# Three 256-column products in place of a 512 and a 256, and a sum taken out by ScalarE alone

## The chip, the cores and the metric

The kernel runs on one core of a Trainium2 chip. The metric is the device time of one execution in microseconds; lower is better. The kernel before takes 1694.68 us in the median of three runs (1694.48 to 1695.0). Numbers of the trace come from one profiled execution of it.

## The reference

One layer of a hybrid decoder trunk on x of 256 positions and 2048 features, all in float32:

```
h = x @ w_in                      # 2048 x 14352, columns for three branches and three gates
y_a = s5_branch(...)              # diagonal complex state space model, then z * sigmoid(z @ w_glu + b_glu)
y_b = gla_branch(...)             # gated linear attention, 4 heads
y_c = hgrn2_branch(...)           # f = lb + (1 - lb) * sigmoid(f_logit), q = silu(q), 8 heads
merged = sum_b sigmoid(gate_b) * (y_b @ w_up_b)
x = layer_norm(alpha * x + merged @ w_out)
x = layer_norm(alpha * x + square(relu(x @ w_mlp_in)) @ w_mlp_out)
```

The hidden width of the MLP is 8192. A layer is done once. Nearly all of the arithmetic lies in the products with the weight matrices.

## The kernel before

**Products in two parts.** Every float32 operand of a large product is split into a coarse part (hi, rounded to the type fp32r) and the rest (lo). A product is the sum of three: hi·hi, hi·lo and lo·hi. ScalarE makes hi by a copy, VectorE makes lo by a subtraction (both 128x1024 elements for one weight tile, L129 and L107 in the profile, since one helper records all activations and one all additions of two tensors).

**Chunks.** The program is a list of chunks, each 512 columns ("rows") or 256 columns ("cols") of one weight matrix. A chunk of kind "rows" keeps positions on the partitions: the activations are the stationary operand and the weights move, 512 columns at a time, in three matmuls (L1327, L1328, L1329). A chunk of kind "cols" gives its result transposed, output columns on partitions and the 256 positions along the bank: the weights are stationary and the activations move. A tile of activations holds hi and lo side by side, 256 columns each, so `a[2]` is both (512 columns), `a[0]` is hi and `a[1]` is lo. One step on 128 rows of the contraction was two matmuls, L1332 and L1333:

```
T.matmul(ps, lhsT=wh[:, i, n], rhs=a[2], start=f, stop=False)
T.matmul(ps[:, 0:256], lhsT=wl[:, i, n], rhs=a[0], start=False, stop=l)
```

The first puts hi·hi into columns 0 to 255 of a PSUM bank and hi·lo into columns 256 to 511; the second adds lo·hi to columns 0 to 255. The two halves still had to be added when the bank was taken out: that is `joined`, a copy of the right half by ScalarE and an addition of the left half by VectorE. A function (Silu, Sigmoid, Relu) followed half a step later on ScalarE, over the tile in SBUF.

**Which chunks are transposed.** The inputs of S5 (four chunks), keys and queries of the GLA branch (two and two), forget gates and queries of the HGRN branch (four and four), all with a contraction of 2048; the four chunks of the S5 gate `w_glu` (contraction 1024); and all of the MLP's first product but its first 512 columns (30 chunks, contraction 2048). A chunk has two result tiles (t = 0 and 1). That makes 100 tiles. One more chunk of kind "low" uses L1332 and L1333 too and is not changed.

**Order.** One loop goes over all steps (a quarter of a chunk's contraction or an eighth, for one t). In each step it first issues splits some steps ahead, takes out finished banks (`evacuate`), issues weight loads, runs side tasks, and then issues the step's matmuls. Side tasks (the S5 scan, the attention of the other branches, what follows a bank taken out) are generators; those of lower priority run only while two running sums, estimated VectorE and ScalarE time (`used["v"]`, `used["s"]`, filled by the helpers `tt`, `stt`, `act` and lowered by 1240 a step), are below zero. So an operation that is no longer issued lets tasks run earlier. Each engine then works off its instructions in the order of issue. Three banks serve as accumulators, five after the S5 scan is done. `joined` took a buffer of the pool of 18 half pages, which the S5 tasks use as well.

Of the kernel before, what the change touches and what calls it, by code (L numbers as in the profile page):

```python
# [55 lines left out]
def trunk_kernel(ctx: ExitStack, tc, io, out):  # L56
# [27 lines left out]
    def half(shape=(128, 2, 256), dt=F32):  # L84
        return take("hf", shape, dt)
# [34 lines left out]
    def act(o, a, f, bias=None, scale=None, accum=None):  # L120
        used["s"] += size(a) / 1.3 + 180
        kw = {}
        if bias is not None:
            kw["bias"] = bias
        if scale is not None:
            kw["scale"] = scale
        if accum is not None:
            kw["accum_out"] = accum
        S.activation(o, a, f, **kw)  # L129
# [590 lines left out]
            act(R[key, c][:, t, :], ps, func, scale=scale)  # L720
        return f

    def joined(ps, o, scale=None):

        b = half((128, 2, 256))
        act(b[:, 0, :], ps[:, 256:512], AF.Copy, scale=scale)
        if scale is None:
            tt(o, ps[:, 0:256], b[:, 0, :], ALU.add)
        else:
            stt(o, ps[:, 0:256], scale, b[:, 0, :], ALU.mult, ALU.add)  # L730
        free(b)

    def ev_page(key, i, func=None, scale=None):

        def f(t, ps):
            n = 2 * i + t
            if n == 0:
                R[key] = page()
            o = R[key][:, n, :]
            joined(ps, o, scale)  # L740

            def later():
                yield 0.5
                if func is not None:
                    act(o, o, func)
                if n == 3:
                    yield 0.5
                    R[key, "ok"] = True
            spawn(later(), -1)
        return f  # L750

    def room(tag, n, reserve=4):
# [69 lines left out]
    def ev_f(g, i):  # L822

        def f(t, ps):
            n = 2 * i + t
            if n == 0:
                R["fA", g], R["fK", g] = page(), page()
            hd = 4 * g + n
            A, K = R["fA", g][:, n, :], R["fK", g][:, n, :]
            joined(ps, K)  # L830

            def later():
                yield 0.5
                act(K, K, AF.Sigmoid)
                yield 0.5
                ts(A, K, S5["oml"][:, hd:hd + 1], S5["lb"][:, hd:hd + 1], ALU.mult, ALU.add)
                ts(K, A, -1.0, 1.0, ALU.mult, ALU.add)
                if n == 3:
                    R["f", g] = True
            spawn(later(), -1)  # L840
        return f
# [176 lines left out]
    def ev_mlp1(hc, i):  # L1018

        def f(t, ps):  # L1020
            n = 2 * i + t
            if n == 0:
                hid[hc] = page(dt=F32R), page(dt=F32R)
            hi, lo = (p[:, n, :] for p in hid[hc])
            a = half()
            h = a[:, 0, :]
            joined(ps, h)

            def later():
                yield 0.5  # L1030
                act(h, h, AF.Relu)
                act(h, h, AF.Square)
                act(hi, h, AF.Copy)
                yield 0.5
                tt(lo, h, hi.bitcast(F32), ALU.subtract)
                free(a)
            spawn(later(), -1)
        return f
# [102 lines left out]
    def ev_glu(c, i):  # L1141
        def f(t, ps):
            n = 2 * i + t
            if n == 0:
                yT.setdefault("A", {})[c] = (page(dt=F32R), page(dt=F32R))
            hi, lo = (p[:, n, :] for p in yT["A"][c])
            sg = half()
            g = sg[:, 0, :]
            joined(ps, g)
            b = 4 * c + n  # L1150

            def later():
                yield 0.5
                act(g, g, AF.Sigmoid, bias=S5["bglu"][:, b:b + 1])
                yield 0.5
                tt(g, g, zT[c][:, n, :], ALU.mult)
                yield 0.5
                act(hi, g, AF.Copy)
                yield 0.5
                tt(lo, g, hi.bitcast(F32), ALU.subtract)  # L1160
                free(sg)
                if c == 1 and n == 3:
                    free(*zT.values())
            spawn(later(), -1)
        return f
# [122 lines left out]
    for s, (c, ku, j, t) in enumerate(steps):  # L1288
        now[0] = s
        if id(c) not in started:  # L1290
            started.add(id(c))
            for f in hooks.get(id(c), []):
                f()
        old = split_n[0]
        early = ln_from - 8 <= s < ln_from + 12
        kept = max(0, 8 - len(x1q)) if early and s >= ln_from else 0
        while (split_n[0] < len(order) and first_use[split_n[0]] <= s + (14 if early else 2 if s < 14 else LA + 4 * (s > 660))
               and len(live["pg"]) + 2 + kept <= limit["pg"]):
            emit_split()
        if early:  # L1300
            emit_lower(split_n[0])
        evacuate()
        fetch()
        run_tasks(1240, 1240)
        emit_lower(old if s >= 10 else split_n[0])
        if s < 14 and t == 1:
            x_piece(s // 2 + 1)
        k = c.index[ku, j]
        if k not in sps:
            emit_split()  # L1310
        emit_lower(k + 1)
        hi, lo = sps[k]
        kpu = c.kpu
        nk = len(c.units) * kpu
        if t not in c.ps:
            c.ps[t] = c.ps[0] if c.kind == "low" and t else accumulator()
        ps = c.ps[t]
        nj = kpu // 2
        wn = c.units[0].shape[2]
        wh, wl = (a.rearrange("p a b -> p (a b)").rearrange("p (k n) -> p k n", n=wn) for a in (hi, lo))  # L1320
        for i in range(nj):
            kt = ku * kpu + j * nj + i
            f, l = kt == 0, kt == nk - 1
            a = c.act(kt)
            if c.kind == "rows":
                sl = slice(t * 128, (t + 1) * 128)
                T.matmul(ps, lhsT=a[0][:, sl], rhs=wh[:, i, :], start=f, stop=False)  # L1327
                T.matmul(ps, lhsT=a[0][:, sl], rhs=wl[:, i, :], start=False, stop=False)  # L1328
                T.matmul(ps, lhsT=a[1][:, sl], rhs=wh[:, i, :], start=False, stop=l)  # L1329
            elif c.kind == "cols" or i // (nj // 2) == t:  # L1330
                n = slice(t * 128, (t + 1) * 128) if c.kind == "cols" else slice(0, 128)
                T.matmul(ps, lhsT=wh[:, i, n], rhs=a[2], start=f, stop=False)  # L1332
                T.matmul(ps[:, 0:256], lhsT=wl[:, i, n], rhs=a[0], start=False, stop=l)  # L1333
        uses_left[k] -= 1
        if uses_left[k] == 0:
            free(*sps.pop(k))
        if ku == len(c.units) - 1 and j == 1 and (c.kind != "low" or t == 1):
            done.append((c, t, ps))
# [55 lines left out]
```

## Time and profile before

| what | value |
|---|---|
| median of three runs | 1694.68 us |
| the profiled execution's own time | 1694.67 us |
| its span, first to last instruction | 1692.9 us |
| granted TensorE clock, mean | 0.996 |
| HBM read | 308.71 MB |
| weight tiles of 512 KB fetched by SyncE from w_in, w_mlp_in, w_mlp_out, w_up, w_out, w_glu | 224, 128, 128, 48, 32, 8 |

The time of the profiled execution is 1.8 us more than its span and 0.01 us under the median. A row of a group of instructions gives: line, engine, operation, output<-input tiles, shapes, count, then busy time in us and mean ns of one, then the idle time of the engine just before them with what ended it. A row of the timeline gives start and length in us. PE is TensorE's matmuls, PEld its weight loads, DVE VectorE, ACT ScalarE. The ends of matmuls are modelled; their starts are what can be compared. `acc` is an accumulator bank, `pg` a page of SBUF, `hf` a half page, `m` and `pb` banks of side tasks.

### The profile page before, as it was taken

Reading aid. Unit: us, or ns where it says so; the run is one execution under the profiler, and the core shown is the slowest. Engines: PE = TensorE matmul, PEld = TensorE weight load, DVE = VectorE, ACT = ScalarE, POOL = GpSimd, SP = SyncE. Lnnn points to the kernel's source line nnn. Section 1 sums busy time; section 2 is a strip of 40 time slices with the busy share of each in tenths; the row PEclk is TensorE's granted clock in tenths of the full one; section 3 lists DMA queues with packets and bytes.
Section 4 is the critical chain, followed back from the end, with each engine's and each line's share of the span. In section 5 each row is a group of like instructions: output and inputs, shape, how many; then the busy total and the mean of one; then the engine's idle time right before and its main releaser. Section 6 shows DMA issues by size and latency. Waiting matters only on the chain.

```text
span 1692.9 us, 24205 instructions
## 1 busy us (share of the span) xinstructions
PE 1669.5 (99%) x9390; PEld 1385.6 (82%) x9390; DVE 1196.9 (71%) x1586; ACT 826.0 (49%) x1166; POOL 166.3 (10%) x121
## 2 busy tenths in 40 slices
PE   8999999999999999999999999999999999999996
PEld 6888888887877877878888888888888888888885
DVE  5978889698999999985675667555455555555556
ACT  4463554464545444435554466454454545454540
POOL 3132211021322322100000000000000000000000
PEclk9999999999999999999999999999999999999998
DMA  9855565555555665766686555656656565656661
GB/s 289 255 160 170 166 178 173 159 166 163 173 179 150 222 188 165 244 199 196 189 278 210 171 162 157 196 178 191 199 187 210 168 207 166 219 173 203 205 216 50
DMA packets 222899, 318.70 MB, mean 188 GB/s; under 512 B 13204, under 2 KB 122128, under 8 KB 222784
## 3 DMA queue, kind: packets, MB, share of 16 engines
q1 hardware_dynamic: 218448, 309.45, 58.6%
q10 hardware_dynamic: 3568, 6.46, 1.3%
q0 software_dynamic: 768, 1.25, 0.5%
q8 instruction: 74, 1.21, 0.3%
q14 instruction: 41, 0.34, 0.1%
HBM read 308.71 MB, written 2.10 MB: 184 GB/s over the span
## 4 chain that ended last, share of the span: by engine, by line
PE 91%; DVE 5%; ACT 1%; DMA 1%; issue 1%; SPq 0%; DVEq 0%; ACTq 0%
PE acc L1332 21%; PE acc L1327 19%; PE acc L1328 19%; PE acc L1329 19%; PE acc L1333 10%; DVE pg L107 2%; DMA pg<-in_w_in_dram 1%; DVE hf L107 1%; PE m L554 1%; ACT pg L129 1%; PE m L134 1%; DVE pg L118 1%; ACT hf L129 1%; PE m L625 1%; PE pb L510 0%
## 5 line engine op out<-in xcount | busy, mean ns | idle before, releaser
L129 ACT ACTIVATE pg<-pg 128x1024 fp32r<-128x1024 f32 (+2 forms) x604 | 603.4, 1028 | 416.5 <-DVE pg L107 131.9
L107 DVE TENSOR_TENSOR pg<-pg,pg 128x1024 fp32r<-128x1024 f32 (+3 forms) x646 | 752.5, 1192 | 65.4 <-ACT pg L129 39.5
L1327 PE MATMUL acc<-pg,pg 128*128 128x512 f32 x1504 | 595.4, 396 | 4.2 <-ACT pg L129 3.6
L1328 PE MATMUL acc<-pg,pg 128*128 128x512 f32 x1504 | 587.7, 391 | 1.1 <-DVE pg L107 1.1
L1329 PE MATMUL acc<-pg,pg 128*128 128x512 f32 x1504 | 587.2, 390 | 0.3 <-DVE pg L107 0.2
L1332 PE MATMUL acc<-pg,pg 128*128 128x512 f32 x1552 | 551.2, 400 | 0.0
L1333 PE MATMUL acc<-pg,pg 128*128 128x256 f32 x1552 | 436.2, 281 | 0.0
L1332 PEld LDWEIGHTS acc<-pg,pg 128*128 128x128 f32 x1552 | 292.2, 188 | 72.4 <-issue 0.7
L1327 PEld LDWEIGHTS acc<-pg,pg 128*128 128x128 f32 x1504 | 282.9, 188 | 68.2 <-issue 5.4
L1329 PEld LDWEIGHTS acc<-pg,pg 128*128 128x128 f32 x1504 | 282.7, 188 | 61.1 <-DVE pg L107 1.1
L1328 PEld LDWEIGHTS acc<-pg,pg 128*128 128x128 f32 x1504 | 283.1, 188 | 59.5 <-DVE pg L107 4.0
L1333 PEld LDWEIGHTS acc<-pg,pg 128*128 128x128 f32 x1552 | 293.9, 189 | 0.7 <-DVE pg L107 0.2
L129 ACT ACTIVATE hf<-acc 128x256 f32<-128x256 f32 (+2 forms) x103 | 39.9, 387 | 186.1 <-PE acc L1333 177.7
L107 DVE TENSOR_TENSOR pg<-pg,acc 128x512 f32<-128x512 f32 x56 | 38.3, 684 | 123.0 <-PE acc L1329 123.0
L107 DVE TENSOR_TENSOR hf<-acc,hf 128x256 f32<-128x256 f32 (+1 forms) x69 | 29.1, 421 | 134.6 <-ACT hf L129 134.6
L107 DVE TENSOR_TENSOR hf<-hf,hf 128x512 f32<-128x512 f32 (+1 forms) x144 | 117.3, 833 | 3.5 <-ACT hf L129 1.4
L129 ACT ACTIVATE hf<-hf 128x256 f32<-128x256 f32 (+1 forms) x152 | 67.7, 455 | 2.1 <-DMA hf<-pg 0.2
L129 ACT ACTIVATE pg<-acc 128x512 f32<-128x512 f32 x40 | 23.8, 594 | 77.9 <-PE acc L1329 77.8
L107 DVE TENSOR_TENSOR hf<-pb,hf 128x256 f32<-128x256 f32 x128 | 46.4, 414 | 19.1 <-PE pb L510 13.3
L107 DVE TENSOR_TENSOR pg<-hf,pg 128x256 fp32r<-128x256 f32 x84 | 34.7, 422 | 27.7 <-ACT pg L129 27.6
L129 ACT ACTIVATE pg<-m 128x512 fp32r<-128x512 f32 (+2 forms) x35 | 19.7, 562 | 66.2 <-PE m L134 47.1
L484 POOL TENSOR_TENSOR hf<-pg 128x512 f32<-128x512 f32 x16 | 19.8, 1238 | 303.4 <-PE pb L510 85.9
(127 smaller groups left out, 665.9 us busy)
## 6 DMA issues: line engine op xcount, KB each, us to landing
pg<-in_w_in_dram SPq DMA_DIRECT2D x224, 512.0 KB, 4.2
pg<-in_w_mlp_in_dram SPq DMA_DIRECT2D x128, 512.0 KB, 4.6
pg<-in_w_mlp_out_dram SPq DMA_DIRECT2D x128, 512.0 KB, 4.1
pg<-in_w_up_dram SPq DMA_DIRECT2D x48, 512.0 KB, 4.7
pg<-in_w_out_dram SPq DMA_DIRECT2D x32, 512.0 KB, 5.1
pg<-in_s_w_glu_dram SPq DMA_DIRECT2D x8, 512.0 KB, 4.8
hf<-pg SPq DMA_DIRECT2D x96, 32.0 KB, 2.1
hf<-hf SPq DMA_DIRECT2D x96, 32.0 KB, 1.9
```

Of the source, the lines that this page charges most:

```text
L107: V.tensor_tensor(o, a, b, op=op)
L118: V.scalar_tensor_tensor(o, a, s, b, op0=op0, op1=op1)
L129: S.activation(o, a, f, **kw)
L134: T.transpose(ps[:, i * 128:(i + 1) * 128], s, ident)
L484: G.tensor_tensor(co, coarse(cs), fine(cs), op=ALU.mult)
L554: T.matmul(yps[r, 0:256], lhsT=W[:, 2 + ri, r], rhs=m[:, i, :], start=ri == 0, stop=ri == 1)
L625: T.matmul(ps[32 * c:32 * c + 32, i * 16:(i + 1) * 16], lhsT=Kf[:, r], rhs=q4[:, :, 1, :], start=True, stop=True)
L1327: T.matmul(ps, lhsT=a[0][:, sl], rhs=wh[:, i, :], start=f, stop=False)
L1328: T.matmul(ps, lhsT=a[0][:, sl], rhs=wl[:, i, :], start=False, stop=False)
L1329: T.matmul(ps, lhsT=a[1][:, sl], rhs=wh[:, i, :], start=False, stop=l)
L1332: T.matmul(ps, lhsT=wh[:, i, n], rhs=a[2], start=f, stop=False)
L1333: T.matmul(ps[:, 0:256], lhsT=wl[:, i, n], rhs=a[0], start=False, stop=l)
```

## The change

In "cols" chunks the step's two matmuls become three of 256 columns, all into columns 0 to 255 of the bank: hi·hi, hi·lo (the same stationary weights `wh` again) and lo·hi. The bank then holds the finished sum in 256 columns, and `joined` is gone: ScalarE takes the tile out of PSUM in one activation with the function it needs, straight to its place. The part of each `later` task that applied the function, and the half step before it, are gone too.

```diff
-    def joined(ps, o, scale=None):
-
-        b = half((128, 2, 256))
-        act(b[:, 0, :], ps[:, 256:512], AF.Copy, scale=scale)
-        if scale is None:
-            tt(o, ps[:, 0:256], b[:, 0, :], ALU.add)
-        else:
-            stt(o, ps[:, 0:256], scale, b[:, 0, :], ALU.mult, ALU.add)
-        free(b)
-
-    def ev_page(key, i, func=None, scale=None):
+    def ev_page(key, i, func=AF.Copy, scale=None):
...
-            o = R[key][:, n, :]
-            joined(ps, o, scale)
...
+            act(R[key][:, n, :], ps[:, 0:256], func, scale=scale)
+            if n == 3:
+                R[key, "ok"] = True
...
-            joined(ps, K)
+            act(K, ps[:, 0:256], AF.Sigmoid)
...
-            joined(ps, h)
+            act(h, ps[:, 0:256], AF.Relu)
 
             def later():
-                yield 0.5
-                act(h, h, AF.Relu)
                 act(h, h, AF.Square)
                 act(hi, h, AF.Copy)
...
-            joined(ps, g)
             b = 4 * c + n
+            act(g, ps[:, 0:256], AF.Sigmoid, bias=S5["bglu"][:, b:b + 1])
...
-                T.matmul(ps, lhsT=wh[:, i, n], rhs=a[2], start=f, stop=False)
-                T.matmul(ps[:, 0:256], lhsT=wl[:, i, n], rhs=a[0], start=False, stop=l)
+                o = ps[:, 0:256]
+                if c.kind == "cols":
+                    T.matmul(o, lhsT=wh[:, i, n], rhs=a[0], start=f, stop=False)
+                    T.matmul(o, lhsT=wh[:, i, n], rhs=a[1], start=False, stop=False)
+                else:
+                    T.matmul(ps, lhsT=wh[:, i, n], rhs=a[2], start=f, stop=False)
+                T.matmul(o, lhsT=wl[:, i, n], rhs=a[0], start=False, stop=l)
```

TensorE at the end of one transposed chunk and the start of the next, with the first matmul group of the S5 scan (L510, into the banks `pb`) between them. In the other rows the first tile after the arrow is a page of activations, the second a page of weights (1053 and 1081 hold hi before, 1195 and 1229 now; the others lo). Before:

```order
L1332 MATMUL acc_1072<-pg_349,pg_1053 128x512
L1333 MATMUL acc_1072<-pg_349,pg_1054 128x256
L510 MATMUL pb_0_1178<-hf_1094,hf_1095 128x256 x2
L510 MATMUL pb_1_1179<-hf_1094,hf_1095 128x256 x2
L1332 MATMUL acc_1200<-pg_111,pg_1081 128x512
L1333 MATMUL acc_1200<-pg_111,pg_1082 128x256
```

And now:

```order
L1310 MATMUL acc_1216<-pg_349,pg_1195 128x256
L1311 MATMUL acc_1216<-pg_349,pg_1195 128x256
L1314 MATMUL acc_1216<-pg_349,pg_1196 128x256
L510 MATMUL pb_0_1346<-hf_1246,hf_1247 128x256 x2
L510 MATMUL pb_1_1347<-hf_1246,hf_1247 128x256 x2
L1310 MATMUL acc_1371<-pg_111,pg_1229 128x256
L1311 MATMUL acc_1371<-pg_111,pg_1229 128x256
L1314 MATMUL acc_1371<-pg_111,pg_1230 128x256
```

Each pair of 512 and 256 columns is a triple of 256; the columns streamed stay 768, the instructions go from two to three, each with its own load of weights. This first group of the scan stands where it stood.

ScalarE, where the two tiles of a chunk of the MLP's first product are taken out. Rows of `pg` from `pg` with 128x1024 are splits of weights, rows from `hf` work on the hidden tile. Before:

```order
L129 ACTIVATE hf_10320<-acc_10241 128x256
L129 ACTIVATE pg_10332<-pg_10231 128x1024
L129 ACTIVATE hf_10336<-acc_10251 128x256
L129 ACTIVATE hf_10319<-hf_10319 128x256 x2
L129 ACTIVATE pg_10317<-hf_10319 128x256
L129 ACTIVATE hf_10335<-hf_10335 128x256 x2
L129 ACTIVATE pg_10317<-hf_10335 128x256
```

And now:

```order
L129 ACTIVATE hf_10975<-acc_10869 128x256
L129 ACTIVATE hf_10975<-hf_10975 128x256
L129 ACTIVATE pg_10973<-hf_10975 128x256
L129 ACTIVATE pg_10992<-pg_10859 128x1024
L129 ACTIVATE hf_10995<-acc_10883 128x256
L129 ACTIVATE hf_10995<-hf_10995 128x256
L129 ACTIVATE pg_10973<-hf_10995 128x256
```

The copy out of the bank and one of the two passes over the hidden tile have become one activation, and the tile's whole work follows at once.

VectorE, where the first weights of the S5 branch are laid out (`s5eb`, `s5ec`; TensorE transposes them next), during the S5 input chunks. Rows of 128x1024 are the lo parts of weight tiles; L592 makes masks. Before:

```order
L107 TENSOR_TENSOR pg_184<-pg_184,hf_801 128x512
L107 TENSOR_TENSOR pg_184<-pg_184,hf_800 128x512
L418 MEMSET s5eb 128x256
L107 TENSOR_TENSOR pg_824<-pg_616,pg_823 128x1024
L107 TENSOR_TENSOR pg_728<-acc_760,hf_856 128x256
L435 COPY s5eb<-pg_184 64x4x16 x2
L112 TENSOR_SCALAR s5ec<-pg_187,gmask 128x2x64
```

And now:

```order
L107 TENSOR_TENSOR pg_184<-pg_184,hf_847 128x512
L107 TENSOR_TENSOR pg_184<-pg_184,hf_846 128x512
L418 MEMSET s5eb 128x256
L107 TENSOR_TENSOR pg_897<-pg_633,pg_896 128x1024
L592 CAST lvl<-hf_192 128x128 x5
L435 COPY s5eb<-pg_184 64x4x16 x2
L112 TENSOR_SCALAR s5ec<-pg_187,gmask 128x2x64
```

The addition out of the bank (`pg_728<-acc_760,hf_856`) is gone. On TensorE the transposes of these tiles stand two steps earlier than before, and the matmul groups of the S5 scan after the first one (L510) mostly 10 to 34 steps earlier, the second group 15 steps later. In both programs ScalarE has 21 loads of function tables, and SyncE and GpSimd issue the same instructions in number.

More of the change, by code (lines that the diff above doesn't have):

```diff
@@ L738, in f @@
                 R[key] = page()
-            o = R[key][:, n, :]
-            joined(ps, o, scale)
-            def later():
-                yield 0.5
[L744 to L749, printed above, removed]
+            act(R[key][:, n, :], ps[:, 0:256], func, scale=scale)
+            if n == 3:
+                R[key, "ok"] = True
         return f
@@ L829, in f @@
             A, K = R["fA", g][:, n, :], R["fK", g][:, n, :]
-            joined(ps, K)
+            act(K, ps[:, 0:256], AF.Sigmoid)
             def later():
-                yield 0.5
-                act(K, K, AF.Sigmoid)
                 yield 0.5
@@ L1026, in f @@
             h = a[:, 0, :]
-            joined(ps, h)
+            act(h, ps[:, 0:256], AF.Relu)
             def later():
-                yield 0.5
-                act(h, h, AF.Relu)
                 act(h, h, AF.Square)
@@ L1148, in f @@
             g = sg[:, 0, :]
-            joined(ps, g)
             b = 4 * c + n
+            act(g, ps[:, 0:256], AF.Sigmoid, bias=S5["bglu"][:, b:b + 1])
             def later():
-                yield 0.5
-                act(g, g, AF.Sigmoid, bias=S5["bglu"][:, b:b + 1])
                 yield 0.5
```

## The prediction

> **What bounds the kernel now.** I read the page first: busy shares, clock, and the chain that ended last.
>
> ```profile
> span 1692.9 us, 24205 instructions
> PE 1669.5 (99%) x9390; PEld 1385.6 (82%) x9390; DVE 1196.9 (71%) x1586; ACT 826.0 (49%) x1166; POOL 166.3 (10%) x121
> PE 91%; DVE 5%; ACT 1%; DMA 1%; issue 1%; SPq 0%; DVEq 0%; ACTq 0%
> ```
>
> TensorE is busy all the time, and 91% of the chain runs over it. Its waits (the view of waits for PE; total in us, times, longest) are small, the longest in total first:
>
> ```profile
> PE acc L1327 <- ACT pg L129: 3.6, 2, 2.4
> ...
> PE m L134 <- DVE s5eb L435: 1.1, 1, 1.1
> ```
>
> So nothing taken from VectorE or ScalarE can bring more than a few microseconds, and what TensorE is given to do decides. The groups of the transposed products:
>
> ```profile
> L1332 PE MATMUL acc<-pg,pg 128*128 128x512 f32 x1552 | 551.2, 400 | 0.0
> L1333 PE MATMUL acc<-pg,pg 128*128 128x256 f32 x1552 | 436.2, 281 | 0.0
> L1333 PEld LDWEIGHTS acc<-pg,pg 128*128 128x128 f32 x1552 | 293.9, 189 | 0.7 <-DVE pg L107 0.2
> ```
>
> L1332 and L1333 never waited: the transposed products run with no gap. Their lengths (400, 281 ns) are no costs, since neighbours overlap; the cost of one is the distance from its start to the next start. Every matmul has its own load of weights, 189 ns long, also overlapped. Of the 1552 pairs 16 belong to the "low" chunk; 1536 change: MLP 30 chunks x 16 rows of the contraction x 2 tiles = 960, S5 gate 4 x 8 x 2 = 64, token mixers 16 x 16 x 2 = 512.
>
> **What a pair costs.** The timeline of PE in transposed chunks of the MLP, the first rows and the last of a stretch:
>
> ```profile
> 1104.77 0.28 PE L1333 MATMUL acc<-pg,pg 128*128 128x256 f32 x1
> 1104.88 0.40 PE L1332 MATMUL acc<-pg,pg 128*128 128x512 f32 x1
> 1105.11 0.28 PE L1333 MATMUL acc<-pg,pg 128*128 128x256 f32 x1
> 1105.23 0.40 PE L1332 MATMUL acc<-pg,pg 128*128 128x512 f32 x1
> ...
> 1139.15 0.40 PE L1332 MATMUL acc<-pg,pg 128*128 128x512 f32 x1
> ```
>
> 96 pairs lie between the starts 1105.23 and 1139.15: 33.92 / 96 = **353.3 ns** a pair. In the mixers the same pairs also run a little faster, here just after an S5 group:
>
> ```profile
> 120.23 0.64 PE L510 MATMUL pb<-hf,hf 96*128 96x256 f32 x4
> 120.71 0.40 PE L1332 MATMUL acc<-pg,pg 128*128 128x512 f32 x1
> ...
> 134.93 0.39 PE L1332 MATMUL acc<-pg,pg 128*128 128x512 f32 x1
> ```
>
> 41 pairs in 14.22 us: 346.8 ns. Both patterns occur in the mixers, so I take 350 ns there and 353.3 in the MLP and the S5 gate.
>
> **What a triple will cost.** Three 256-column matmuls in a row, each with new weights, do not occur in L1332/L1333, but the S5 groups L510 are four such in a row, of the same type. The first row above and these (start of the group, start of what follows it):
>
> ```profile
> 265.28 0.64 PE L510 MATMUL pb<-hf,hf 96*128 96x256 f32 x4
> 265.75 0.40 PE L1332 MATMUL acc<-pg,pg 128*128 128x512 f32 x1
> ...
> 705.07 0.64 PE L510 MATMUL pb<-hf,hf 96*128 96x256 f32 x4
> 705.55 0.40 PE L1327 MATMUL acc<-pg,pg 128*128 128x512 f32 x1
> ```
>
> Four matmuls take 0.48, 0.47 and 0.48 us: 1.43 / 12 = 0.1192, between 0.117 and 0.12 each. The 512-column ones alone, from the stretch of "rows" chunks behind them:
>
> ```profile
> 1152.15 0.39 PE L1327 MATMUL acc<-pg,pg 128*128 128x512 f32 x1
> ...
> 1167.79 0.39 PE L1327 MATMUL acc<-pg,pg 128*128 128x512 f32 x1
> ```
>
> 69 steps in 15.64 us: 226.7 ns. So 256 more columns cost 107 ns, and about 12 ns of each matmul do not depend on its width. That is the point of the change on TensorE: the columns stay 768, and this fixed part is paid three times instead of twice. From these pieces a pair is 226.7 + 119.2 = 346 ns, as in the faster pattern, and a triple 3 x 119.2 = 357.6 ns. With two of three groups at 0.12 I take 0.1195, **358.5 ns** a triple.
>
> - MLP and S5 gate: 1024 x (358.5 - 353.3) = +5.3 us.
> - Mixers: 512 x (358.5 - 350) = +4.4 us.
>
> Can the third load of weights bind? One row of loads of 128x128 weights that follow each other without a wide matmul:
>
> ```profile
> 315.53 0.97 PEld L640 LDWEIGHTS m<-pg,pg 128*128 128x128 f32 x8 [0.56 <-issue]
> ```
>
> Eight loads in 0.97 us, the last of them 0.19 long: (0.97 - 0.19) / 7 = 0.111 us from one to the next. That is below 0.1195, so the load fits under a 256-column matmul, with 8 ns to spare; in the pair the 512 left far more.
>
> **What goes from the other engines.** The groups that read the bank, and the functions behind them:
>
> ```profile
> L129 ACT ACTIVATE hf<-hf 128x256 f32<-128x256 f32 x120 | 49.4, 412 | 1.9
> L129 ACT ACTIVATE hf<-acc 128x256 f32<-128x256 f32 x100 | 38.3, 383 | 177.5 <-PE acc L1333 174.3
> L107 DVE TENSOR_TENSOR hf<-acc,hf 128x256 f32<-128x256 f32 x68 | 28.6, 421 | 134.6 <-ACT hf L129 134.6
> L107 DVE TENSOR_TENSOR pg<-acc,hf 128x256 f32<-128x256 f32 x28 | 11.7, 418 | 11.1 <-ACT hf L129 11.1
> ```
>
> VectorE loses 68 + 28 additions and four more with a scale: 100 x 0.42 = 42 us. ScalarE keeps its 100 reads of a bank, now with the function in them, and loses the separate functions of 84 tiles (60 Relu, 16 Sigmoid or Silu, 8 gate Sigmoid), 84 x 0.41 = 35 us. A function on a bank should cost what the copy did (383 ns against 412 from SBUF). The cover of all this is TensorE: both engines worked under it, and the ends of transposed tiles stood before nobody (idle of L1332: 0.0). I cost it at nothing. If that cover were gone, 42 us would be the most that it could be worth.
>
> What can show is one place where VectorE is late and TensorE stands:
>
> ```profile
> 92.38 0.28 PE L1333 MATMUL acc<-pg,pg 128*128 128x256 f32 x1
> 93.75 0.44 PE L134 MATMUL m<-ident,s5eb 128*128 128x128 f32 x2 [1.09 <-DVE s5eb L435]
> 95.12 0.44 PE L134 MATMUL m<-ident,s5ec 128*128 128x128 f32 x2 [0.94 <-DVE s5ec L112]
> 95.31 0.65 PE L1332 MATMUL acc<-pg,pg 128*128 128x512 f32 x1
> ...
> 95.97 0.63 PE L1332 MATMUL acc<-pg,pg 128*128 128x512 f32 x1
> ...
> 39.50:142.90 103.40, 101.38 (x566) 87.22 (x565) 88.85 (x142) 57.34 (x77) 21.01 (x14) 0.98 0.69 210
> ```
>
> (The last row is the view by windows; its 0.98 is the granted clock.) TensorE waits 1.09 + 0.94 us there, and behind it a pair takes 0.66 us instead of 0.35 for a while, at a lowered clock: 0.02 x 103.4 = about 2 us more. But the order shows that these transposes stand two steps (2.8 us) earlier now, about what the additions ahead of them on VectorE free; and later scan groups come 10 to 34 steps earlier, on a VectorE that is 88.85 / 103.40 = 86% busy here, ahead of the lo parts for which TensorE may wait. Bounds: 4 us gained, 4 us lost; I take -1 us.
>
> No new wait arises at the banks: a bank is read once, by the same ScalarE instruction in the same place of its queue, and is free one VectorE addition sooner. The tables that functions need are loaded 21 times in both orders.
>
> **Sum.** 1694.67 (the profiled execution's own time, 0.01 under the median) + 5.3 + 4.4 - 1 = **1703.4 us**.
>
> **The rivals.**
>
> *No change: the extra step costs no more than the pair's own 256.* L1333's start to the next L1332 is 0.11 and 0.12 us in the rows above. With 0.1175 a triple is 352.5 ns: 1024 x -0.8 + 512 x 2.5 = +0.5 us, with the -1 us 1694.2; this case spans 1691.3 to 1698. Against it: that start is followed by a 512, whose distance then is 0.23 to 0.24, more than the 0.227 of its kind, so the 0.1175 is only half of a shifted pair. A rule of the Trainium skill, "TensorE: Matmul & The Clock Gate", section "Back-to-back issue gap", goes the same way: a matmul costs its columns plus 2.5 ns, which as an estimate is +2.5 ns a triple, +3.8 us in all, 1697.5 with the -1. The trace's fixed part of 12 ns, with weights changed each time, does not agree with its 2.5.
>
> *Faster: equal widths run tighter.* If the irregular pattern (353.3 against 346) is a price of alternating widths and the step falls to the mean of 0.11 and 0.12, a triple is 345 ns: 1024 x -8.3 + 512 x -5 = -11.1 us, 1682.6. It decides as soon as a step is under 0.117. Against it: no L510 group shown is under 0.47.
>
> *Slower: the excess stays.* If the 7 ns by which MLP pairs exceed their pieces (353.3 - 346) come with the accumulation in one region and stay with each triple, it costs 365.5 ns: 1024 x 12.2 + 512 x 15.5 = +20.4 us, 1714.1 with the -1. For it: L510 does not accumulate, and its stationary rows are 96, not 128. Against it: "rows" triples accumulate too and are at the plain 226.7.
>
> **Chances.** The forecast, 1699 to 1710: 0.60. No change: 0.15. Faster: 0.09. Slower by the excess, 1710 to 1718: 0.16. The range, 1692 to 1715, leaves out the faster case and the top of the slower one. A measurement of this kernel tells 0.2% (3.4 us) from no change: faster than 1691.3 has 0.10, between 0.15, slower than 1698.1 0.75.
>
> **What would show it.** In the timeline of the changed kernel's MLP chunks, 96 triples in 34.4 us (no change: 33.9; slower: 35.1), three starts 0.119 to 0.12 apart. No row of TensorE's view of waits goes over 4 us. VectorE's busy time is about 42 us less and ScalarE's 35 us less with the span no shorter. The prediction is wrong if a step leaves 0.117 to 0.1215, or if waits of L1310 on lo parts appear between 100 and 380 us.

## The result, and the profile after

The changed kernel takes **1710.28 us** in the median of four runs (1708.74 to 1712.0), against 1694.58 us (1694.2 to 1695.0) for the kernel before on the same chip: a ratio of 1.0096, 95% interval 1.0084 to 1.0109. It is slower, by 15.7 us. The forecast was 1703.4 with a range of 1692 to 1715: right in direction, and 6.9 us short in size. The run that was profiled is the lowest of the four: 1708.74 us, 14.1 more than the profiled run of before. Executions of one kernel differ by up to 4 us here: in the series of the experiments those of before lie either at 1692.6 to 1693.3 or at 1694.0 to 1696.1, and the profiled one, 1694.67, belongs to the upper group; so a difference under 2 us between two single traces decides nothing by itself.

The head of the page after, and its chain that ended last:

```profile
span 1707.0 us, 27135 instructions
PE 1680.6 (98%) x10926; PEld 1468.9 (86%) x10926; DVE 1162.6 (68%) x1486; ACT 795.3 (47%) x1082; POOL 160.4 (9%) x121
PE 64%; DVE 4%; ACT 1%; issue 1%; DVEq 0%
```

VectorE has 100 instructions less and is busy 34 us less, ScalarE 84 and 31 us, in a span 14 us longer. (Where a view gives shares, each step back in the chain picks one releaser; its PE share is no busy time.) TensorE now has 1536 matmuls more, which are the third of each triple:

```profile
L1314 PE MATMUL acc<-pg,pg 128*128 128x256 f32 x1552 | 439.2, 283 | 0.0
L1310 PE MATMUL acc<-pg,pg 128*128 128x256 f32 x1536 | 436.2, 284 | 0.0
L1311 PE MATMUL acc<-pg,pg 128*128 128x256 f32 x1536 | 434.6, 283 | 0.0
```

The triples never wait either (idle 0.0). The timeline of PE in the MLP, the first rows and the last of 97 triples:

```profile
1112.74 0.28 PE L1310 MATMUL acc<-pg,pg 128*128 128x256 f32 x1
1112.86 0.28 PE L1311 MATMUL acc<-pg,pg 128*128 128x256 f32 x1
1112.98 0.28 PE L1314 MATMUL acc<-pg,pg 128*128 128x256 f32 x1
1113.10 0.28 PE L1310 MATMUL acc<-pg,pg 128*128 128x256 f32 x1
...
1147.66 0.28 PE L1310 MATMUL acc<-pg,pg 128*128 128x256 f32 x1
```

(1147.66 - 1112.74) / 97 = **360.0 ns** a triple, three steps of 0.12 us each, against 353.3 ns for a pair. That is the first part of the loss. The second stands in the view of waits for PE (total, times, longest):

```profile
PE acc L1303 <- ACT pg L129: 3.5, 2, 2.3
PE acc L1303 <- DVE pg L107: 3.4, 3, 2.6
PE m L134 <- DVE s5eb L435: 3.3, 1, 3.3
```

The wait for `s5eb` has grown from 1.1 us, and one of 2.6 us is new. It lies in a stretch that has no transposed chunk at all. The timeline of PE there:

```profile
509.20 0.39 PE L1305 MATMUL acc<-pg,pg 128*128 128x512 f32 x1
512.18 0.79 PE L1303 MATMUL acc<-pg,pg 128*128 128x512 f32 x1 [2.59 <-DVE pg L107]
512.77 0.63 PE L1304 MATMUL acc<-pg,pg 128*128 128x512 f32 x1
```

VectorE's timeline, at the same place:

```profile
507.15 3.24 DVE L107 TENSOR_TENSOR hf<-hf,hf 128x512 f32<-128x512 f32 x2
510.31 1.21 DVE L107 TENSOR_TENSOR pg<-pg,pg 128x1024 fp32r<-128x1024 f32 x1
511.45 0.68 DVE L107 TENSOR_TENSOR pg<-acc,pg 128x512 f32<-128x512 f32 x1
```

And GpSimd's:

```profile
506.11 2.04 POOL L488 TENSOR_TENSOR hf<-pg,pg 128x512 f32<-128x512 f32 x1
508.23 1.61 POOL L489 TENSOR_TENSOR hf<-hf,hf 128x512 f32<-128x512 f32 x1
```

TensorE waits for a bank that VectorE reads (`pg<-acc,pg`, the product with the gate, at 511.45). Ahead of that read stand two additions of the S5 scan, 3.24 us long beside GpSimd, and a split. When the bank comes, the clock is down: the view by windows (us, busy of each engine, PEclk, DMA share, GB/s) grants 0.53 for the next 3.5 us.

```profile
512.10:515.60 3.50, 3.42 (x9) 2.70 (x9) 3.45 (x10) 1.06 (x1) 0.00 (x0) 0.53 0.01 2
```

Before, the same two additions took as long, 7.4 us earlier. VectorE's row in before:

```profile
499.73 3.25 DVE L107 TENSOR_TENSOR hf<-hf,hf 128x512 f32<-128x512 f32 x2
```

And the step of PE in before that waited behind them; it needed only the split, and lost 0.41 us:

```profile
504.17 0.50 PE L1328 MATMUL acc<-pg,pg 128*128 128x512 f32 x1 [0.41 <-DVE pg L107]
```

So the S5 scan's groups have moved against the chunks, and one now stands ahead of a bank.

**Where the time went.** The large matmuls fall into stretches of transposed and of "rows" chunks in the same sequence in all kernels here. This table gives, in us, how much longer each stretch is than before in the one profiled execution (from the start of its first large matmul to that of the next stretch; the times in its head are those of before). The sum is the difference of the spans. The experiments of the next section stand in it too.

| kernel | first mixers 39.5-142.9 | other mixers 220.7-272.7, 327.3-377.3 | "rows" 377.3-807.9 | gate and MLP, from 807.9 | the rest | sum |
|---|---|---|---|---|---|---|
| the changed kernel | +2.1 | +2.1 | +4.5 | +6.5 | -1.1 | +14.1 |
| e1 three products, evacuation kept | +0.2 | +2.4 | 0.0 | +5.6 | -0.2 | +8.0 |
| e2 evacuation alone | +2.3 | -0.1 | +4.5 | 0.0 | +0.4 | +7.2 |
| e3 tasks held back by estimates | +4.2 | +0.4 | +7.6 | +6.5 | +0.7 | +19.4 |
| e6 tasks in their old places | +4.2 | +2.6 | 0.0 | +6.5 | -0.8 | +12.4 |
| e8 MLP alone | -0.3 | 0.0 | -0.1 | +6.1 | +1.8 | +7.5 |
| e9 as e6, GpSimd held | -1.9 | +2.6 | -0.1 | +6.5 | -0.9 | +6.2 |
| e10 before, GpSimd held | -2.1 | 0.0 | 0.0 | 0.0 | -0.2 | -2.3 |
| e12 changed kernel, GpSimd held | -1.5 | +2.1 | +4.5 | +6.5 | +1.3 | +13.0 |
| e4 before, widths grouped | -0.3 | +0.1 | 0.0 | -2.9 | 0.0 | -3.1 |
| e11 as e4, GpSimd held | -2.6 | +0.1 | 0.0 | -2.9 | -0.2 | -5.5 |
| e5 before, one "rows" product split | 0.0 | 0.0 | +6.1 | +5.5 | +4.4 | +15.9 |

In e2, e3, e8 and e12, 1.5 to 1.8 us of "the rest" lie before 39.5 us, where no part of the change works (in e5 2.8 us). In these five the granted clock between 29.5 and 33.5 us, behind a wait for split weights, was 0.62 to 0.88; in before, the changed kernel and the others it was 1.00. So the sums of these five rows are about that much too high for their edits.

### The profile page after: what moved, and what is told of

The parts are those of the page before. It is cut to its first block, busy times and chain, and to the rows that moved or that the text cites. A ratio compares the mean times of both kernels' runs of the same rounds, so it can differ in the third digit from the quotient of the medians.

```text
span 1707.0 us, 27135 instructions
## 1 busy us (share of the span) xinstructions
PE 1680.6 (98%) x10926; PEld 1468.9 (86%) x10926; DVE 1162.6 (68%) x1486; ACT 795.3 (47%) x1082; POOL 160.4 (9%) x121
## 4 chain that ended last, share of the span: by engine, by line
PE 64%; DVE 4%; ACT 1%; issue 1%; DVEq 0%
PE acc L1303 14%; PE acc L1304 14%; PE acc L1305 14%; PE acc L1314 7%; PE acc L1311 7%; PE acc L1310 7%; DVE pg L107 2%; DVE hf L107 1%; DVE pg L118 1%; ACT hf L129 1%; PE m L134 0%; ACT pg L129 0%; PE m L554 0%; DVE hf L534 0%; PE pb L510 0%
## 5 line engine op out<-in xcount | busy, mean ns | idle before, releaser
L107 DVE TENSOR_TENSOR pg<-pg,pg 128x1024 fp32r<-128x1024 f32 (+2 forms) x646 | 747.6, 1190 | 90.7 <-ACT pg L129 61.3
L129 ACT ACTIVATE pg<-pg 128x1024 fp32r<-128x1024 f32 (+1 forms) x588 | 597.6, 1044 | 421.8 <-PE acc L1304 146.5
L1303 PE MATMUL acc<-pg,pg 128*128 128x512 f32 x1504 | 596.1, 396 | 7.0 <-ACT pg L129 3.5
L1304 PE MATMUL acc<-pg,pg 128*128 128x512 f32 x1504 | 587.8, 391 | 1.1 <-DVE pg L107 1.1
L1305 PE MATMUL acc<-pg,pg 128*128 128x512 f32 x1504 | 587.4, 391 | 0.3 <-DVE pg L107 0.2
L1314 PE MATMUL acc<-pg,pg 128*128 128x256 f32 x1552 | 439.2, 283 | 0.0
L1310 PE MATMUL acc<-pg,pg 128*128 128x256 f32 x1536 | 436.2, 284 | 0.0
L1311 PE MATMUL acc<-pg,pg 128*128 128x256 f32 x1536 | 434.6, 283 | 0.0
L1303 PEld LDWEIGHTS acc<-pg,pg 128*128 128x128 f32 x1504 | 283.4, 188 | 71.7 <-issue 5.4
L1305 PEld LDWEIGHTS acc<-pg,pg 128*128 128x128 f32 x1504 | 283.1, 188 | 61.1 <-DVE pg L107 1.1
L1304 PEld LDWEIGHTS acc<-pg,pg 128*128 128x128 f32 x1504 | 283.6, 189 | 58.4 <-DVE pg L107 2.9
L1314 PEld LDWEIGHTS acc<-pg,pg 128*128 128x128 f32 x1552 | 297.8, 192 | 0.0
L1310 PEld LDWEIGHTS acc<-pg,pg 128*128 128x128 f32 x1536 | 294.8, 192 | 1.8 <-issue 1.2
L1311 PEld LDWEIGHTS acc<-pg,pg 128*128 128x128 f32 x1536 | 294.8, 192 | 0.5
L107 DVE TENSOR_TENSOR hf<-hf,hf 128x512 f32<-128x512 f32 (+1 forms) x144 | 111.7, 794 | 3.4 <-ACT hf L129 1.4
L129 ACT ACTIVATE pg<-acc 128x512 f32<-128x512 f32 (+1 forms) x72 | 36.0, 500 | 144.3 <-PE acc L1305 93.2
L129 ACT ACTIVATE hf<-acc 128x256 f32<-128x256 f32 (+2 forms) x63 | 24.1, 383 | 149.6 <-PE acc L1314 144.3
L534 DVE TENSOR_TENSOR_SCAN hf<-p,hf 128x256 f32<-128x256 f32 x64 | 48.9, 809 | 0.0
L484 POOL TENSOR_TENSOR hf<-pg 128x512 f32<-128x512 f32 x16 | 19.5, 1219 | 311.1 <-PE pb L510 93.1
```

The source lines that it names most:

```text
L107: V.tensor_tensor(o, a, b, op=op)
L484: G.tensor_tensor(co, coarse(cs), fine(cs), op=ALU.mult)
L534: V.tensor_tensor_scan(z[:, i, :], S5["mag"][:, j:j + 1].to_broadcast([128, 256]), z[:, i, :], 0.0, ALU.mult, ALU.add)
L1310: T.matmul(o, lhsT=wh[:, i, n], rhs=a[0], start=f, stop=False)
L1311: T.matmul(o, lhsT=wh[:, i, n], rhs=a[1], start=False, stop=False)
L1314: T.matmul(o, lhsT=wl[:, i, n], rhs=a[0], start=False, stop=l)
```

## The experiments

Two theories stood first. One: the loss is the third matmul, so much for each triple. The other: the evacuation's lighter work moves the tasks, and the loss is waits. e1 has the first without the second, e2 the second without the first.

**e1: three products, the old evacuation.** In the kernel before; the first row of each tile stays a pair, and hi·lo still goes to the right half.

```diff
-                T.matmul(ps, lhsT=wh[:, i, n], rhs=a[2], start=f, stop=False)
...
+                if c.kind == "cols" and not f:
+                    T.matmul(o, lhsT=wh[:, i, n], rhs=a[0], start=False, stop=False)
+                    T.matmul(ps[:, 256:512], lhsT=wh[:, i, n], rhs=a[1], start=False, stop=False)
+                else:
+                    T.matmul(ps, lhsT=wh[:, i, n], rhs=a[2], start=f, stop=False)
...
```

> The kernel before with three 256-column products a row of the contraction (but the first row of each tile), hi.lo into the right half of the bank, so that the copy and the addition stay; the side tasks stand where they stood. My theory (about 12 to 13 ns of every matmul do not depend on its width): 1436 more matmuls; MLP and gate 956 x 6.7 = +6.4 us, mixers 480 x 10 = +4.8 us, so 1705.8 us, and a triple is 0.360 us. Rival (the time comes from the new way out of the bank or the moved tasks): 1694.6 us.

Measured: 1702.72 us against 1694.46, ratio 1.0053 (1.0038 to 1.0068), +8.2 us, 3.1 us less than its theory's 1705.8. The matmuls stand 0.12 us apart as in the changed kernel, TensorE's side tasks stand between the same chunks as in before, and so do the waits at the S5 transposes; the one at 510 us does not come. But the half clock that follows the transposes in before does not follow here, so the first mixers grow by 0.2 us only; gate and MLP grow by 5.6 us where 6.4 were forecast. So the third matmul accounts for somewhat over half of the loss, and whether hi·lo goes to its own half of the bank or to the same one makes no difference to the step.

**e2: the new evacuation, the old pair.** In the changed kernel, hi·lo again goes to columns 256 to 511, which nothing reads, so the result leaves that product out.

```diff
...
-                if c.kind == "cols":
-                    T.matmul(o, lhsT=wh[:, i, n], rhs=a[0], start=f, stop=False)
-                    T.matmul(o, lhsT=wh[:, i, n], rhs=a[1], start=False, stop=False)
...
+                T.matmul(ps, lhsT=wh[:, i, n], rhs=a[2], start=f, stop=False)
+                T.matmul(ps[:, 0:256], lhsT=wl[:, i, n], rhs=a[0], start=False, stop=l)
```

> The changed kernel with the old pair of matmuls; ScalarE takes the left half of the bank alone, so the product hi.lo is left out of the result. Side tasks stand as in the changed kernel. My theory: pairs of 0.347 to 0.353 us as before, and only what the moved tasks cost is left (up to 4 us, a wait near 500 us with a lowered clock after it): 1694 to 1699 us. Rival (the freed VectorE and ScalarE time is worth something): under 1691 us.

Measured: 1700.18 against 1694.46, ratio 1.0034 (1.0021 to 1.0046), +5.7 us, 1.2 us above the upper end of its theory. Less work for two engines, the same on the third, and a slower kernel. Both waits of the changed kernel are there in its view of waits for PE:

```profile
PE m L134 <- DVE s5eb L435: 3.8, 1, 3.8
PE acc L1303 <- DVE pg L107: 3.4, 3, 2.6
```

8.2 + 5.7 = 13.9 us: the two parts nearly add up to the whole.

**e8: the change in the MLP alone.** The S5 scan is over there, so none of its tasks is left to move.

```diff
-            joined(ps, h)
+            act(h, ps[:, 0:256], AF.Relu)
...
+                if c.kind == "cols" and c.three:
```

> The change in the MLP's first product alone (960 triples, 60 tiles taken out by one activation with Relu); the rest as before, tasks in their old places. My theory: 960 x 6.7 ns = +6.4 us, 1700.9 us, and nothing for the freed VectorE and ScalarE time there. Rival (the freed time is worth something in the MLP): under 1699 us.

Measured: 1700.71 against 1692.85, ratio 1.0045 (1.0032 to 1.0057): 0.2 us from its theory's 1700.9, but 7.9 us above this series' median of before, which lies in the lower group. The trace gives +0.86 us for each stretch of 128 triples, 6.7 ns a triple, and nothing for the removed additions and functions: 960 x 6.7 = 6.4 us. The "rows" stretches between them change by under 0.05 us each but for the last.

**e3: the tasks held back.** If tasks cause the waits by running too early, entering the removed operations into the estimates should undo them.

```diff
+    def as_before():
+        used["v"] += 256 / 0.96 + 80
+        used["s"] += 256 / 1.3 + 180
...
+            as_before()
...
```

> The changed kernel, with the sums of estimated VectorE and ScalarE time raised as if copy, addition and function were still issued, so that the S5 groups stand within 20 steps behind their old places and not up to 34 ahead. My theory: the wait of 2.6 us at 509 us and the half clock behind it go, 1705 to 1707 us. Rival (the wait has another cause): 1710 us as the changed kernel.

Measured: 1713.79 against 1694.46, ratio 1.0117 (1.0102 to 1.0132). A miss, and slower still. The S5 groups stood 2 to 20 steps from their places of before even so, because the half step that the functions had waited was gone too (e6, which keeps it, restores the places); the wait for a bank near 510 us stayed (2.6 us, at 513 us here), and another of 1.1 us came at 477 us. "Too early" was the wrong word. What counts is which chunk a group meets.

**e6: every task in its old place.** Estimates and half steps are both kept, so that TensorE's side tasks stand exactly where they stood before.

```diff
             act(R[key][:, n, :], ps[:, 0:256], func, scale=scale)
...
+            used["v"] += 256 / 0.96 + 80
+            def later():
+                yield 0.5
+                if func != AF.Copy:
+                    used["s"] += 256 / 1.3 + 180
...
```

> The changed kernel whole, with the estimates and the half steps of the removed operations kept, so that every side task stands on TensorE exactly where it stood before the change. My theory (the changed kernel loses its last 5 to 6 us to the moved tasks): 1700 to 1704 us, no wait of 2.6 us in the stretch of 380 to 815 us, and the wait at the first S5 transposes (2.0 us before) not longer than it was. Rival (the new way out of the bank costs it): 1708 us or more.

Measured: 1707.89 against 1692.85, ratio 1.0089 (1.0075 to 1.0103). Again a miss in the time, but with half an answer: the wait at 510 us is gone (column 377.3-807.9: 0.0 instead of +4.5), so it came from the places of the tasks. The waits at the first S5 transposes are not gone; e6's view of waits for PE has 3.6 us, where before has 1.1 + 0.9:

```profile
PE m L134 <- DVE s5eb L435: 2.6, 2, 2.0
...
PE m L134 <- DVE s5ec L112: 1.0, 1, 1.0
```

Nothing on TensorE differs there but the triples. VectorE's timeline in e6:

```profile
92.24 1.15 DVE L435 COPY s5eb<-pg 64x64 f32<-64x64 f32 x2
93.31 1.36 DVE L112 TENSOR_SCALAR s5ec<-pg,gmask 128x128 f32<-128x128 f32 x1
94.69 1.98 DVE L435 COPY s5eb<-pg 64x64 f32<-64x64 f32 x2
96.70 1.34 DVE L112 TENSOR_SCALAR s5ec<-pg,gmask 128x128 f32<-128x128 f32 x1
```

And GpSimd's in e6:

```profile
91.20 2.04 POOL L485 TENSOR_TENSOR hf<-pg 128x512 f32<-128x512 f32 x1
93.32 1.28 POOL L486 TENSOR_TENSOR hf<-hf,hf 128x512 f32<-128x512 f32 x1
94.55 1.05 POOL L487 TENSOR_TENSOR hf<-pg,pg 128x512 f32<-128x512 f32 x1
95.56 1.05 POOL L488 TENSOR_TENSOR hf<-pg,pg 128x512 f32<-128x512 f32 x1
96.69 1.26 POOL L489 TENSOR_TENSOR hf<-hf,hf 128x512 f32<-128x512 f32 x1
```

The four VectorE operations that the transposes wait for end at 93.39, 94.67, 96.67 and 98.04 us; each end is within 0.2 us of the end of a GpSimd operation (93.24, 94.60, 96.61, 97.95). So each of them ended only as a GpSimd operation ended. The Trainium skill, "SBUF — State Buffer", section "Who interferes with whom", says that a copy or tensor-scalar operation of VectorE in its two-port form and a GpSimd operation exclude each other for a whole instruction; this trace agrees, though no view tells in which form the four operations ran. In before, GpSimd computed a first set of tables (L484 to L489) and then stood for 2.3 us before the second. Its row in before names the releaser:

```profile
91.57 1.06 POOL L484 TENSOR_TENSOR hf<-pg 128x512 f32<-128x512 f32 x1 [2.31 <-DVE pg L107]
```

The releaser is this addition of `joined`, in VectorE's timeline of before, which ends at 91.50. The only half page that it touches is that of `joined`, and GpSimd's output is a half page:

```profile
91.09 0.41 DVE L107 TENSOR_TENSOR pg<-acc,hf 128x256 f32<-128x256 f32 x1
```

In e6 the second set follows the first without a gap:

```profile
89.73 1.51 POOL L484 TENSOR_TENSOR hf<-pg 128x512 f32<-128x512 f32 x1
```

e1 and e8, which keep `joined` here, have the gap of 2.3 us as before. The new theory: the half pages of `joined` had held GpSimd, and without them it runs its second set right where VectorE has small urgent work.

**e9, e10, e12: GpSimd held back.** One tiny write by VectorE to the buffer of the second set makes GpSimd wait for VectorE's place in the order. e9 is e6 with it, e12 the changed kernel, e10 the kernel before.

```diff
         so, co, w = (half((128, 2, 16, 16)) for _ in range(3))
+        if hb == 1:
+            V.memset(co[:, 0, 0, 0:1], 0.0)
         G.tensor_tensor(co, coarse(cs), fine(cs), op=ALU.mult)
```

> As e6 (the changed kernel, tasks in place), and GpSimd's second set of S5 tables held back by one VectorE memset of 128x1 that stands behind the first s5eb and s5ec in VectorE's queue. New theory: without the buffers of the removed addition GpSimd starts that set at 89.7 us instead of 91.6, and VectorE's s5eb and s5ec copies beside it take 1.1 to 2.0 us instead of 0.3, so TensorE waits 3.6 us there. Held back: the copies take 0.3 each and the wait falls under 1 us; the time is 3 to 5 us below e6, 1703 to 1705 us where the kernel before has 1693. Rival (another cause): as e6.

> The changed kernel with the hold alone, tasks where the change put them. Theory: GpSimd's first two sets ran back to back from about 74 to 93 us and VectorE's mask casts took 4.7 us beside them; held back, the wait of 3.3 us at s5eb falls under 1.5 us, while the wait of 2.6 us at 509 us stays: 2 to 4 us below the changed kernel, 1705 to 1708 us where the kernel before has 1694. Rival: 1710 us.

> The kernel before with the same hold alone. Theory: GpSimd starts at 91.57 us there and slows three of the four copies (1.1 to 1.2 us instead of 0.3), TensorE waits 2.0 us; held back, the wait falls under 0.5 us and the time by 1.5 to 4 us (the half clock behind the wait may go too). Rival (the copies are slow by themselves): no change.

All three against 1694.08 us. e9: 1702.06 (1701.05 to 1702.68), ratio 1.0050 (1.0036 to 1.0064), 1 us below the forecast's 1703 to 1705. VectorE's timeline in e9:

```profile
91.50 0.27 DVE L435 COPY s5eb<-pg 64x64 f32<-64x64 f32 x2
91.70 0.27 DVE L112 TENSOR_SCALAR s5ec<-pg,gmask 128x128 f32<-128x128 f32 x1
91.98 0.30 DVE L435 COPY s5eb<-pg 64x64 f32<-64x64 f32 x2
92.31 0.29 DVE L112 TENSOR_SCALAR s5ec<-pg,gmask 128x128 f32<-128x128 f32 x1
```

And where GpSimd's second set begins in e9:

```profile
117.53 1.06 POOL L486 TENSOR_TENSOR hf<-pg 128x512 f32<-128x512 f32 x1 [27.86 <-DVE hf L485]
```

GpSimd is held for far longer than needed (27.9 us), but the four operations take 1.1 us instead of 5.8, and TensorE's rows show no wait for `s5eb` or `s5ec`. In the first mixers e9 is 6.1 us shorter than e6. e9 has all the triples and neither wait, and it is still slower than before: its +6.2 us are the widths less what before itself loses at this place.

e12: 1707.35 (1704.56 to 1707.91), ratio 1.0078 (1.0065 to 1.0090), as forecast: the `s5eb` wait goes (3.6 us in the first mixers), the one at 510 us stays. The changed kernel's wait is not e6's, though. There GpSimd's second set is over at 92.98 us, and the four operations, from 92.99 us on, take 1.1 us. Ahead of them stand the five casts of masks, which the kernel before runs at 55.8 us in 0.75 us. VectorE's timeline in the changed kernel:

```profile
88.39 4.68 DVE L592 CAST lvl<-hf 128x128 uint8<-128x128 f32 x5
```

And in e12, with GpSimd held:

```profile
88.45 0.75 DVE L594 CAST lvl<-hf 128x128 uint8<-128x128 f32 x5
```

So the cause is the same, GpSimd beside VectorE, but it works on other operations, which the change had moved there.

e10: 1692.55, ratio 0.9995 (0.9986 to 1.0004). The profiled execution is 2.3 us shorter, but it lies in the lower group (8 of e10's 11 do, 9 of before's 20), and the interval leaves open whether the kernel before gains anything: a wait of 1.7 us on VectorE's L118 takes the place of those removed (view of waits for PE in e10):

```profile
PE acc L1334 <- DVE pg L118: 1.7, 1, 1.7
```

**e4: equal widths together.** This asks where the 7 ns come from by which a pair exceeds its pieces. It is the kernel before with the four wide matmuls of a step first, then its four narrow ones.

```diff
...
+            for i, kt in enumerate(kts):
+                T.matmul(ps, lhsT=wh[:, i, n], rhs=c.act(kt)[2], start=kt == 0, stop=False)
+            for i, kt in enumerate(kts):
+                T.matmul(ps[:, 0:256], lhsT=wl[:, i, n], rhs=c.act(kt)[0], start=False, stop=kt == nk - 1)
...
```

> The kernel before, with the four 512-column matmuls of a step first and its four 256-column ones after them; nothing else. If the 7 ns by which an MLP pair (353.3 ns) exceeds its pieces (226.7 + 120) come from alternating widths, a pair is 347 to 349 ns and the time 1686 to 1689 us. Rival (the excess belongs to the transposed pair in any order): 1694.6 us.

Measured: 1691.72 against 1694.46, ratio 0.9985 (0.9976 to 0.9994), between the two expectations. The timeline of PE in the MLP:

```profile
1124.89 1.09 PE L1325 MATMUL acc<-pg,pg 128*128 128x512 f32 x4
1125.81 0.64 PE L1327 MATMUL acc<-pg,pg 128*128 128x256 f32 x4
1126.29 1.09 PE L1325 MATMUL acc<-pg,pg 128*128 128x512 f32 x4
```

Four wide ones take 0.92 us, 0.23 each, not 0.2267; four narrow ones 0.48. A wide matmul that follows a wide one is still slower here, so the excess doesn't come from the change of width at each step alone. e11 is e4 with GpSimd held:

> e4 (four wide matmuls of a step first, then the four narrow ones) with the hold: the two gains add, 3 to 6 us below the kernel before. Rival (the hold is worth nothing): 2.7 us below, as e4.

Measured: **1689.21** us (1689.09 to 1690.99) against 1694.08, ratio 0.9976 (0.9967 to 0.9985). It is faster than both kernels, by 4.9 us against before.

**e5: the same extra matmuls elsewhere.** In "rows" chunks one of three 512-column products is split into two of 256 (not in a tile's first row); the evacuations stay.

```diff
-                T.matmul(ps, lhsT=a[0][:, sl], rhs=wh[:, i, :], start=f, stop=False)
+                for q in range(0, 512, 512 if f else 256):
...
```

> The kernel before, with one of the three 512-column matmuls of the kind rows split into two of 256 columns (but for the first of each tile): 1366 more matmuls, same columns. My theory (a fixed 13.3 ns in every matmul, whichever operand is the weight): +18.2 us, 1712.7 us. If each 256-column step amid 512-column ones costs the 6.7 ns more that the pair showed, twice 6.7 are added: 1731 us. Rival (the fixed part belongs to the transposed products): 1694.6 us.

Measured: 1709.05 against 1692.85, ratio 1.0092 (1.0079 to 1.0106): 16.2 us for 1366 extra matmuls, 11.9 ns each in the net, 2 us less than expected. The pairs, which e5 doesn't touch, became faster; PE's timeline in its MLP:

```profile
1123.71 0.39 PE L1333 MATMUL acc<-pg,pg 128*128 128x512 f32 x1
...
1126.14 0.39 PE L1333 MATMUL acc<-pg,pg 128*128 128x512 f32 x1
```

Seven pairs in 2.43 us: 347 ns, in the MLP, where before has 353.3. Behind 39.5 us the transposed stretches of e5 are 5.5 us shorter than before, and the "rows" stretches 18.6 us longer for 1336 extra matmuls: 13.9 ns each on average, near the theory's 13.3. The average hides a spread: 11.4 ns in the stretch from 377 to 808 us, 18 ns in those of the MLP (1.02 us for 56). So no single fixed part describes all places.

## Why the prediction was right in direction and short in size

| term | forecast | measured in the traces |
|---|---|---|
| MLP and S5 gate, width | +5.3 | +6.5 |
| mixers, width | +4.4 | +4.2 to +4.7 |
| relief of VectorE and ScalarE | -1 | +2.9 to +3.4 (what is left) |
| sum | +8.7 | +14.1 |

- **TensorE bounds, the columns stay, a fixed part is paid three times.** Shown in direction: e1 loses by the triples alone, e8's loss lies in its stretches of triples, and e5 loses by extra matmuls at another place. The size is not one number: an extra matmul cost 6.7 ns in the MLP's triples, 10.2 in those of the later mixers (1.31 us for 128), 11.4 to 18 in e5.
- **The triple.** Taken 358.5 ns, measured 360.0. Of the three short L510 groups two had given 0.12 and one 0.117 each, and I averaged them; the long chain is at 0.12 throughout. For 1024 triples that is 1.5 us, against a miss of 1.2 in the term.
- **The mixers.** 350 ns as a mean of two patterns was good. e9 gives +1.3 in each of the two later stretches. In the first, before loses about 4.0 us at the transposes (92.38 to 95.31 is 2.45 us more than the 0.48 that e9 takes there, and then five pairs at 0.65 instead of 0.35), e9 nothing, and it is 1.9 shorter: 2.1 us of width. That makes 4.7; the same for e1, where the half clock does not follow, makes 4.2 to 4.3.
- **The step that failed: relief "-1 us", and "No new wait arises at the banks".** That sentence weighed the banks of the transposed tiles. The new wait came at a bank of a "rows" chunk, which VectorE reads: a scan group that the change had moved put two additions ahead of that read. With the half clock behind it this is worth +4.5 us, most of the 5.4 us by which the traces exceed the forecast. The prediction gave ±4 us for moved groups and looked for waits on lo parts between 100 and 380 us. Those did not come, and no row of the view of waits exceeds 4 us, as it said. The transposes at 92 us did not gain by standing 2.8 us earlier either. The forecast let the removed additions free VectorE there, but five mask casts had come to stand in their place (VectorE's order ahead of the prediction has them), and beside GpSimd they took 4.68 us. So 2.0 us of waits became 3.3; in time the place costs 3.7 us where before loses 4.0, since the clock stays up. The prediction had asked what a removed *operation* frees. It had not asked what the removed *buffer* had held back: GpSimd's second set of tables. e2 shows that the evacuation costs 5.7 us by itself, e6 that the places of the tasks make the wait at 510 us, e9 and e12 that GpSimd's overlap makes the one at 92.
- **What relief did bring.** Behind the +4.5 and the -0.3 at the transposes about -1.1 us is left over; 0.8 of it lies between 272.7 and 327.3 us, where before waits 0.8 us for VectorE at 286 us and the changed kernel does not. VectorE's busy time fell by 34 us and ScalarE's by 31, where 42 and 35 were forecast; the mask casts alone took 3.9 us more.
- **Work off the path at nothing.** Right for the MLP (e8: the triples explain all), wrong where tasks share the engines.
- **The rivals.** "No change" and "faster" fell: no step left 0.12. "The excess stays" (365.5 ns) fell as well, by the 360.0 ns. Yet the time came out 0.3 us outside the 1699 to 1710 that the prediction gave to its own mechanism, and inside the band of this rival. That is an accident of the wait at 510 us; and that the range, 1692 to 1715, holds the time is in part luck, since its slower end stood there for another mechanism. The fixed cost of a matmul, by the steps of 120.0 and 226.7 ns, is 2 x 120.0 - 226.7 = 13.3 ns, where 12 was taken. The 2.5 ns of the Trainium skill, "TensorE: Matmul & The Clock Gate", section "Back-to-back issue gap", which that section gives for an isolated matmul, and the 1697.5 worked out from it do not hold here.

The four runs' median lies 1.5 us above the profiled one. No trace covers that difference, and it stays open; it is of the size that five other profiled executions lost before 39.5 us at a lowered clock. Open too is 0.4 us of the first mixers' +2.1 (2.1 of width, 3.7 lost at the transposes instead of 4.0).

## What to carry to other kernels

Where TensorE is busy all the time, count its matmuls and not only their columns: here an extra one for the same columns cost 7 to 18 ns, so splitting a wide product to save work on engines off the path was a loss. Before taking away an operation that "costs nothing", list what waits for its buffers and whose place in the order it fixes; what runs earlier then may meet an urgent step on a shared resource. The remedy found here was not more relief but one deliberate dependence that keeps GpSimd away from a few small VectorE operations. It took 6.1 us from the first mixers of e6 and 3.6 from those of the changed kernel; for the kernel before, alone, a gain is not shown.

## What the runs showed of the hardware that was not expected

- **VectorE beside GpSimd.** Four small VectorE operations took 1.1 us together with GpSimd idle (e9) and 5.8 with it at work (e6); two 128x512 additions took 3.24 us instead of 1.27; five casts took 4.68 us instead of 0.75.
  The shorter row, of VectorE in before at a time when GpSimd stood still (the longer ones, beside GpSimd, are in the section on the result):

```profile
493.97 1.27 DVE L107 TENSOR_TENSOR hf<-hf,hf 128x512 f32<-128x512 f32 x2
```

- **An idle of 3.3 us may cost less than one of 2.6.** In the changed kernel the clock stays at 1.00 behind the 3.3 us at 92 us, and falls to half behind the 2.6 us at 510; e1 waits for the same transposes as long as before (1.0 + 0.9 us) and has no half clock behind them, while before has it. In e2 the same wait is 3.8 us long and the clock behind it is 0.55 for 3 us. The view by windows, in the changed kernel behind the wait:

```profile
92.00:96.00 4.00, 2.19 (x14) 1.87 (x15) 3.95 (x9) 1.38 (x2) 0.98 (x1) 1.00 0.00 0
```

  In before:

```profile
96.00:99.00 3.00, 3.00 (x11) 2.56 (x11) 3.00 (x5) 2.08 (x3) 1.26 (x1) 0.52 0.14 38
```

  In e1:

```profile
96.00:99.00 3.00, 3.00 (x26) 2.95 (x25) 3.00 (x4) 2.49 (x3) 0.64 (x1) 1.00 0.07 16
```

  The Trainium skill, "TensorE: Matmul & The Clock Gate", section "What's actually happening", describes a window of 3.4 us that runs by itself, whatever the kernel does. That fits a loss that depends on where the idle time falls; its threshold of a whole idle window does not fit the 2.6 us.
- **The same pairs ran at two rates.** A 512-column matmul in a long chain takes 226.7 ns from start to start. A pair takes 353.3 ns in the MLP of before and 347 in that of e5, with the same instructions, though only the "rows" chunks between them differ. What carries over from one stretch to the next was not found.
